# Local attention in a two-layer hybrid backbone: a score matmul of 64 partitions becomes one of 128

## The chip, the cores and the metric

The kernel runs on one core of one Trainium2 chip. The metric is the device time of one execution in microseconds (us). The kernel before took 3382.59 us (median of three runs, 3379.35 to 3383.43).

## What is computed

Two layers over 1152 tokens (1024 latent tokens on a grid and 128 context tokens, model width 1024). Each layer normalises and modulates its input, projects it once, runs three mixers side by side (a gated linear recurrence, a latent attention called MLA below, and a windowed attention called SWA or local attention), merges them through gates and adds the result to the residual. The change lies in the scores of the local attention of the latent tokens:

```python
def swa_latent(q, k, v, k_ctx, v_ctx, sink):
    ...
    def block(args):
        n, q_b = args
        start = n * BLOCK
        k_b = lax.dynamic_slice_in_dim(kp, start, 3 * BLOCK, axis=1)
        ...
        k_all = jnp.concatenate([k_b, k_ctx], axis=1)
        ...
        s = jnp.einsum("bqhgd,bkhd->bhgqk", q_b, k_all).astype(jnp.float32) * scale
        s = jnp.where(valid, s, NEG_INF)
        pr = sink_softmax(s, sink).astype(v.dtype)
        return jnp.einsum("bhgqk,bkhd->bqhgd", pr, v_all)
```

A query block of 128 tokens sees its own block of keys, the one before, the one after (masked to a band of 128) and the 128 context keys. There are 8 query heads of 64 channels, in two groups of four that share a key head. Context tokens attend to context tokens alone.

## The kernel before, in words

Every product is made in float32r from two parts: a value x is split into a high part xh (a cast to float32r) and a low part xl = x - xh. Most products are then three matmuls that add into one PSUM tile (`mm3`, line 239). The local attention does it with two, since its channel count, 64, is half of the 128 partitions. Keys are put side by side twice before they are transposed, so a transposed key tile `skt` holds the same 64 channels in partitions 0 to 63 and again in 64 to 127. `kprep_ops` (lines 1320 to 1343) writes the high parts of both halves to `KH[g]` on ScalarE (line 1337; the tile is `skh` in the profile) and the low parts of the lower half alone to `KL[g]` on VectorE (line 1341, `skl`). Its three steps are called `kp`, `ka`, `kb`. `qprep_ops` does it otherwise for the queries: the tile `qt` holds qh in partitions 0 to 63 and ql in 64 to 127 (lines 1351 to 1361).

`soft_ops(n, g)` makes the scores of query block n (0 to 8, of which 8 is the context block) and key head g. Its step `s0` to `s3` (function `mm`, lines 1379 to 1392) makes one head's scores in a PSUM tile `ss`. For each run of neighbouring key blocks it issues

- line 1388: `qt` (all 128 partitions) times `KH`, which is qh*kh + ql*kh;
- line 1389: `qt[0:64]` times `KL[0:64]`, which is qh*kl;
- line 1391: for each edge block a 128x128 matmul of the identity with the mask.

Blocks n = 1 to 5 have two runs, one of 384 columns with two masks and one of 128 columns (the context keys); block 0 has 256 with one mask and 128; block 6 has one run of 512 with two masks; block 7 one of 384 with one mask; block 8 one of 128. Over 8 heads and 2 layers these are 144 score steps with 240 matmuls of line 1388 and 240 of line 1389: 96 of 384 columns, 16 of 512, 16 of 256 and 112 of 128. In the profile the shape of a matmul is written rows*columns of the stationary operand and then rows x columns of the moving one, so line 1389 reads `64*128 64x384`.

After a score step VectorE takes the row maximum (`r`, line 1397) and bounds it by the sink (`b`, line 1401), ScalarE makes the exponentials (`x`, line 1406), VectorE and ScalarE make the inverse sums (`z1` to `z4`), and GpSimd scales the weights (`n`, line 1411). Then TensorE transposes them (`T`, line 1437), ScalarE and VectorE split them (`h`, line 1441, and `l`, line 1445), and TensorE multiplies them with the values (`V`, lines 1450 and 1451). Between these steps stand merge matmuls of the MLA branch (`m` and `e`, tile `mg`, line 239).

The order of all these steps on TensorE, ScalarE, VectorE and GpSimd is written out by hand, in the strings `MS_ORDER` (line 51, from the last MLA heads into the local attention) and `S_ORDER` (line 77, one turn per query block and key head), and the scheduler may not move them (line 1591). Three `ss` tiles are in turn.

Of the kernel before, what the change touches and what calls it, by code (L numbers as in the profile page):

```python
# [12 lines left out]
ALU = mybir.AluOpType  # L13
# [178 lines left out]
def _backbone(ctx, tc, nc, a, depth):  # L192
# [11 lines left out]
    def f(x):  # L204
        return x.bitcast(F32)
# [295 lines left out]
    for l in range(depth):  # L501
# [384 lines left out]
        with ExitStack() as ast:  # L886
# [197 lines left out]
            def w_ops(h):  # L1084
                r = []
                r.append(("uq", h, a["w_uq"][l, h], 3, P))
                if h and h % 2 == 0:
                    r.append(("uk", h // 2, a["w_uk"][l, h // 2], 2, P))
                if h in (0, 5):
                    r.append(("uv", h // 5, a["w_uv"][l, h // 5], 2, 256))  # L1090
                raws = []

                def load():
                    for nm, i, src, nk, n in r:
                        raws.append(wraw(src, nk, n, f"{nm}{l}_{i}"))

                def hi():
                    for (nm, i, src, nk, n), raw in zip(r, raws):
                        st[nm, i] = whl(nk, n, f"{nm}{l}_{i}")
                        nc.scalar.copy(out=st[nm, i][0], in_=raw)  # L1100

                def lo():
                    for (nm, i, src, nk, n), raw in zip(r, raws):
                        wh, wl = st[nm, i]
                        nc.gpsimd.tensor_tensor(out=wl, in0=raw, in1=f(wh), op=ALU.subtract)
                return {"w": hi, "wl": lo}, load
# [152 lines left out]
            for u in range(32):  # L1259
                h, pr = u // 4, u % 4  # L1260
                o = score_ops(h, pr)
# [13 lines left out]
            for h in (0, 1):  # L1275
                o, load = w_ops(h)
# [6 lines left out]
            KH, KL, VV = [None] * 2, [None] * 2, [None] * 2  # L1283
# [19 lines left out]
            def k_load(i):  # L1303
                if i > 7:
                    return
                kk = box["sqa"].tile([P, 512], F32, tag="kk", name=f"kk{l}_{i}", bufs=3)
                kraw_s[i] = kk
                if i > 4:
                    kk = kk.rearrange("p (t e) -> p t e", t=4)
                    if i < 7:  # L1310
                        nc.sync.dma_start(out=kk, in_=kv_d[4 * i - 20:4 * i - 16].rearrange("t p e -> p t e")[:, :, P:2 * P])
                    for t in (8, 9) if i == 7 else ():
                        nc.sync.dma_start(out=kk[:, t - 8], in_=kv_src(t)[1])
                    return
                kk = kk.rearrange("p (t g r e) -> p t g r e", t=2, g=2, r=2)
                for t in range(2):
                    for e in range(2):
                        nc.sync.dma_start(out=kk[:, t, :, e, :], in_=kv_src(K_OF[i] + t)[0].rearrange("p (g e) -> p g e", g=2))

            def kprep_ops(i):  # L1320
                r = {}
                cs = slice(K_OF[i] * P, (K_OF[i] + 2) * P)

                def mm():
                    r["ps"] = psd.tile([P, 512], F32, tag="d", name=f"skt{l}_{i}")
                    for g in range(2):
                        for e in range(2):
                            o = (2 * g + e) * P
                            nc.tensor.transpose(r["ps"][:, o:o + P], kraw_s[i][:, 256 * e + 128 * g:256 * e + 128 * g + 128], ident)
                    k_load(i + 3)  # L1330

                def hi():
                    for g in range(2):
                        if i == 0:
                            KH[g] = kkp.tile([P, 1280], F32R, tag=f"kh{g}", name=f"skh{l}_{g}")
                            KL[g] = kkp.tile([P, 1280], F32R, tag=f"kl{g}", name=f"skl{l}_{g}")
                        nc.scalar.copy(out=KH[g][:, cs], in_=r["ps"][:, 256 * g:256 * g + 256])

                def lo():
                    for g in range(2):  # L1340
                        nc.vector.tensor_tensor(out=KL[g][0:64, cs], in0=r["ps"][0:64, 256 * g:256 * g + 256],
                                                in1=f(KH[g][0:64, cs]), op=ALU.subtract)
                return {"kp": mm, "ka": hi, "kb": lo}

            def qprep_ops(t, g):
# [18 lines left out]
            def blocks_of(n):  # L1364
                return [b for b in (n - 1, n, n + 1) if 0 <= b < 8] + [8] if n < 8 else [9]

            def soft_ops(n, g):
                blocks = blocks_of(n)
                w = len(blocks) * P
                r, pts = {}, []  # L1370
                soft[n, g] = pts
                runs = []
                for i, b in enumerate(blocks):
                    if runs and runs[-1][1] + runs[-1][2] == b:
                        runs[-1][2] += 1
                    else:
                        runs.append([i, b, 1])

                def mm(j):
                    s = box["ps"].tile([P, 512], F32, tag="s", name=f"ss{l}_{n}_{4 * g + j}", bufs=3)  # L1380
                    r["s", j] = s
                    q = qt[n, g][:, j * P:(j + 1) * P]
                    for i, b, cnt in runs:
                        o = s[:, i * P:(i + cnt) * P]
                        ks = slice(b * P, (b + cnt) * P)
                        msk = [(ii, blocks[ii]) for ii in range(i, i + cnt)
                               if n < 8 and blocks[ii] < 8 and abs(blocks[ii] - n) == 1]
                        nc.tensor.matmul(o, q, KH[g][:, ks], start=True, stop=False)
                        nc.tensor.matmul(o, q[0:64], KL[g][0:64, ks], start=False, stop=not msk)
                        for z, (ii, bb) in enumerate(msk):  # L1390
                            nc.tensor.matmul(s[:, ii * P:(ii + 1) * P], ident_r, mask[:, 0 if bb == n - 1 else 1, :],
                                             start=False, stop=z == len(msk) - 1)

                def rmax(j):
                    if j == 0:
                        r["mx"] = box["sqa"].tile([P, 4, 4], F32, tag="mx", name=f"smx{l}_{n}_{g}", bufs=4)
                    nc.vector.tensor_reduce(out=r["mx"][:, 0, j:j + 1], in_=r["s", j][:, 0:w], axis=AX.X, op=ALU.max)

                def low(j):
                    h, mx = 4 * g + j, r["mx"]  # L1400
                    nc.vector.tensor_scalar(out=mx[:, 0, j:j + 1], in0=mx[:, 0, j:j + 1], scalar1=box["snk"][:, h:h + 1],
                                            scalar2=-1.0, op0=ALU.max, op1=ALU.mult)

                def exp(j):
                    pt = box["sqa"].tile([P, 512], F32, tag="pt", name=f"spt{l}_{n}_{4 * g + j}", bufs=12)
                    nc.scalar.activation(out=pt[:, 0:w], in_=r["s", j][:, 0:w], func=ACT.Exp, bias=r["mx"][:, 0, j:j + 1],
                                         accum_out=r["mx"][:, 1, j:j + 1])
                    pts.append(pt)

                def norm(j):  # L1410
                    nc.gpsimd.tensor_scalar(out=pts[j][:, 0:w], in0=pts[j][:, 0:w], scalar1=r["mx"][:, 3, j:j + 1],
                                            scalar2=1.0, op0=ALU.mult, op1=ALU.mult)

                o = {
                    "z1": lambda: nc.vector.tensor_tensor(out=r["mx"][:, 2], in0=box["snk"][:, 4 * g:4 * g + 4], in1=r["mx"][:, 0], op=ALU.add),
                    "z2": lambda: nc.scalar.activation(out=r["mx"][:, 2], in_=r["mx"][:, 2], func=ACT.Exp),
                    "z3": lambda: nc.vector.tensor_tensor(out=r["mx"][:, 1], in0=r["mx"][:, 1], in1=r["mx"][:, 2], op=ALU.add),
                    "z4": lambda: nc.vector.reciprocal(out=r["mx"][:, 3], in_=r["mx"][:, 1]),
                }
                for t, fn_ in (("s", mm), ("r", rmax), ("b", low), ("x", exp), ("n", norm)):  # L1420
                    o.update({f"{t}{j}": lambda fn_=fn_, j=j: fn_(j) for j in range(4)})
                return o
# [503 lines left out]
```

## Time and profile before

| | before |
|---|---|
| median of three runs | 3382.59 us (3379.35 to 3383.43) |
| profiled execution, first to last instruction | 3375.3 us |
| mean granted TensorE clock | 0.984 |
| TensorE matmuls busy | 3287.6 us (97%) |
| TensorE weight loads busy | 3095.7 us (92%) |
| VectorE busy | 1820.3 us (54%) |
| ScalarE busy | 1551.6 us (46%) |
| GpSimd busy | 1450.9 us (43%) |
| local attention of layer 0, first to last score matmul | from about 1335 to 1538 us |
| the same in layer 1 | from about 2979 to 3177 us |

The profiled execution's own device time is not listed apart from the three runs; they lie 4 to 8 us above its span, which is what lies around the first and the last instruction. A matmul's time in the profile runs until its results are written and overlaps with the next matmul's, so the pace of TensorE is read from the distance between two starts, not from the busy time. PE is TensorE's matmul row, PEld its row of weight loads.

### The profile page before, as it was taken

Reading aid. Unit: us, or ns where it says so; the run is one execution under the profiler, and the core shown is the slowest. Engines: PE = TensorE matmul, PEld = TensorE weight load, DVE = VectorE, ACT = ScalarE, POOL = GpSimd, SP = SyncE. Lnnn points to the kernel's source line nnn. Section 1 sums busy time; section 2 is a strip of 40 time slices with the busy share of each in tenths; the row PEclk is TensorE's granted clock in tenths of the full one; section 3 lists DMA queues with packets and bytes.
Section 4 is the critical chain, followed back from the end, with each engine's and each line's share of the span. In section 5 each row is a group of like instructions: output and inputs, shape, how many; then the busy total and the mean of one; then the engine's idle time right before and its main releaser. Section 6 shows DMA issues by size and latency. Waiting matters only on the chain. (4 is left out here: it accounts for less than half of the span.)

```text
span 3375.3 us, 52189 instructions
## 1 busy us (share of the span) xinstructions
PE 3287.6 (97%) x19572; PEld 3095.7 (92%) x19572; DVE 1820.3 (54%) x3254; ACT 1551.6 (46%) x3061; POOL 1450.9 (43%) x1174
## 2 busy tenths in 40 slices
PE   7999999999999999999999999999999999999998
PEld 4999999999998998778989999999999999977898
DVE  6345443332327888667563444423332588876766
ACT  4344444434226777554243433333341477765532
POOL 3655554433214444445374445333331244434543
PEclk9999999999999999899999999999999999989999
DMA  5333232232441002446432222222244200234563
GB/s 209 100 99 97 95 119 92 94 99 94 153 155 30 25 25 68 125 135 229 169 114 91 77 79 81 81 73 82 85 132 135 86 28 27 51 103 119 171 201 134
DMA packets 246652, 351.06 MB, mean 104 GB/s; under 512 B 73216, under 2 KB 200832, under 8 KB 246144
## 3 DMA queue, kind: packets, MB, share of 16 engines
q1 hardware_dynamic: 246400, 347.74, 32.5%
q8 instruction: 154, 2.52, 0.3%
q14 instruction: 98, 0.80, 0.1%
HBM read 248.88 MB, written 98.78 MB: 103 GB/s over the span
## 5 line engine op out<-in xcount | busy, mean ns | idle before, releaser
L239 PE MATMUL in<-hhi,wh_in 128*128 128x384 f32 x1536 | 524.0, 341 | 6.0 <-ACT osg L734 4.4
L239 PE MATMUL in<-hli,wh_in 128*128 128x384 f32 x1536 | 522.6, 340 | 1.6 <-DVE hli L427 1.6
L239 PE MATMUL in<-hhi,wl_in 128*128 128x384 f32 x1536 | 521.9, 340 | 0.0
L215 POOL TENSOR_TENSOR wl_in<-wr_in,wh_in 128x1024 fp32r<-128x1024 f32 x94 | 235.4, 2506 | 329.3 <-ACT wh_in L209 254.1
L239 PEld LDWEIGHTS in<-hhi,wh_in 128*128 128x128 f32 x1536 | 290.0, 189 | 6.8 <-ACT osg L734 5.0
L239 PEld LDWEIGHTS in<-hli,wh_in 128*128 128x128 f32 x1536 | 289.8, 189 | 3.9 <-DVE hli L427 3.9
L239 PEld LDWEIGHTS in<-hhi,wl_in 128*128 128x128 f32 x1536 | 289.9, 189 | 0.0
L239 PE MATMUL in<-hlh,wh_in 128*128 128x384 f32 x768 | 261.6, 341 | 2.8 <-DVE hlh L427 2.8
L239 PE MATMUL in<-hhh,wl_in 128*128 128x384 f32 x768 | 261.3, 340 | 2.0 <-POOL wl_in L215 2.0
L239 PE MATMUL in<-hhh,wh_in 128*128 128x384 f32 x768 | 261.5, 340 | 0.3 <-ACT osg L734 0.3
L1169 POOL TENSOR_SCALAR p<-p,mx 128x1152 f32<-128x1152 f32 x128 | 158.2, 1236 | 200.9 <-DVE mx L1166 126.4
L1220 DVE TENSOR_TENSOR pl<-pt,ph 128x512 fp32r<-128x512 f32 (+1 forms) x320 | 201.4, 636 | 29.8 <-ACT ph L1216 27.1
L1216 ACT CAST ph<-pt 128x512 fp32r<-128x512 f32 (+1 forms) x320 | 170.1, 552 | 92.4 <-PE pt L1209 87.9
L610 DVE SCALAR_TENSOR_TENSOR r<-r,txl 128x1156 f32<-128x1156 f32 x16 | 31.4, 1962 | 320.9 <-ACT r L609 320.9
L1209 PE MATMUL pt<-ident,p 128*128 128x128 f32 x1152 | 169.7, 274 | 9.5 <-DVE kl L1079 4.1
L734 ACT ACTIVATE osg<-in 128x384 f32<-128x384 f32 x144 | 69.0, 489 | 237.3 <-PE in L239 154.9
L1209 PEld LDWEIGHTS pt<-ident,p 128*128 128x128 f32 x1152 | 133.2, 141 | 32.6 <-DVE pl L1220 10.5
L209 ACT CAST wh_in<-wr_in 128x1024 fp32r<-128x1024 f32 x96 | 99.9, 1044 | 126.2 <-PE in L239 91.6
L1234 PE MATMUL o<-ph,v 128*128 128x256 f32 x576 | 153.2, 293 | 0.0
L239 PEld LDWEIGHTS in<-hlh,wh_in 128*128 128x128 f32 x768 | 145.0, 189 | 4.3 <-DVE hlh L427 4.3
L239 PEld LDWEIGHTS in<-hhh,wl_in 128*128 128x128 f32 x768 | 144.9, 189 | 2.3 <-POOL wl_in L215 2.3
L1234 PE MATMUL o<-pl,v 128*128 128x256 f32 x576 | 145.7, 280 | 0.0
(451 smaller groups left out, 9652.5 us busy)
## 6 DMA issues: line engine op xcount, KB each, us to landing
wr_in<-in_w_fm SPq DMA_DIRECT2D x96, 512.0 KB, 3.6
sg<-osg SPq DMA_DIRECT2D x144, 192.0 KB, 1.9
wr_wm<-in_w_mod SPq DMA_DIRECT2D x32, 512.0 KB, 4.0
wr_wo<-in_w_out SPq DMA_DIRECT2D x32, 512.0 KB, 3.7
yr<-gsil SPq DMA_DIRECT2D x16, 576.0 KB, 2.8
msgrnn<-sg SPq DMA_DIRECT2D x48, 192.0 KB, 2.4
u<-msgrnn SPq DMA_DIRECT2D x48, 192.0 KB, 2.5
qr<-qs SPq DMA_DIRECT2D x36, 256.0 KB, 3.9
```

Of the source, the lines that this page charges most:

```text
L209: nc.scalar.copy(out=hi, in_=src)
L215: eng.tensor_tensor(out=lo, in0=src, in1=f(hi), op=ALU.subtract)
L239: nc.tensor.matmul(ps, x, y, start=n == 0, stop=n == last)
L610: nc.vector.scalar_tensor_tensor(out=rr[d], in0=rr[d], scalar=1.0, in1=tt[d], op0=ALU.add, op1=ALU.mult)
L734: nc.scalar.activation(out=o, in_=ps, func=ACT.Sigmoid)
L1169: nc.gpsimd.tensor_scalar(out=pts[i], in0=pts[i], scalar1=mxs[i][:, 5:6], scalar2=1.0, op0=ALU.mult, op1=ALU.mult)
L1209: nc.tensor.transpose(ps[:, w:w + P], pts[q][:, k * P:(k + 1) * P], ident)
L1216: nc.scalar.copy(out=r["h", j][:, 0:width(j)], in_=r["t", j][:, 0:width(j)])
L1220: nc.vector.tensor_tensor(out=r["l", j][:, 0:width(j)], in0=r["t", j][:, 0:width(j)], in1=f(r["h", j][:, 0:width(j)]), op=ALU.subtract)
L1234: nc.tensor.matmul(O[:, 0:256], V[k][:, h % 4, :], x[:, 256 * i:256 * i + 256], start=k == 0 and e == 0, stop=k == 8 and e == 1)
```

## The change

The low parts of the keys are written to all 128 partitions of `KL`, and the second score matmul takes all 128 partitions of the queries and of `KL`. As both halves of the key tile are the same channels, the second matmul then gives qh*kl + ql*kl; the term ql*kl was left out before.

```diff
                 def lo():
                     for g in range(2):
-                        nc.vector.tensor_tensor(out=KL[g][0:64, cs], in0=r["ps"][0:64, 256 * g:256 * g + 256],
-                                                in1=f(KH[g][0:64, cs]), op=ALU.subtract)
+                        nc.vector.tensor_tensor(out=KL[g][:, cs], in0=r["ps"][:, 256 * g:256 * g + 256],
+                                                in1=f(KH[g][:, cs]), op=ALU.subtract)
...
                         nc.tensor.matmul(o, q, KH[g][:, ks], start=True, stop=False)
-                        nc.tensor.matmul(o, q[0:64], KL[g][0:64, ks], start=False, stop=not msk)
+                        nc.tensor.matmul(o, q, KL[g][:, ks], start=False, stop=not msk)
```

No instruction is added, removed or moved on any engine. What differs in the order of VectorE is the shape of the 20 subtractions of line 1341, here the first two of layer 0 in the last MLA heads (`skl` are the low parts, `qt` the queries, `mx` the row maxima of the MLA softmax):

```order
 L1361 TENSOR_TENSOR qt_0_0_12829<-sqt_0_0_12824,qt_0_0_12829 64x512
-L1341 TENSOR_TENSOR skl_0_12850<-skt_0_12839,skh_0_12849 64x256
-L1341 TENSOR_TENSOR skl_1_12853<-skt_0_12839,skh_1_12852 64x256
+L1341 TENSOR_TENSOR skl_0_12850<-skt_0_12839,skh_0_12849 128x256
+L1341 TENSOR_TENSOR skl_1_12853<-skt_0_12839,skh_1_12852 128x256
 L1146 TENSOR_REDUCE mx_7_1_0_12817<-sm_8907 128x1
```

They stand in the same place and now take 128 partitions of 256 elements instead of 64.

## Rows read from the trace of the kernel before

**Rows 1.** The page: the span, and the granted clock in 40 equal slices, in tenths.

```profile
span 3375.3 us, 52189 instructions
...
PEclk9999999999999999899999999999999999989999
```

**Rows 2.** Busy time by stretch, both local attentions: start:end, length, engines, granted clock, DMA.

```profile
1335.00:1538.00 203.00, 203.00 (x1046) 160.30 (x1045) 139.98 (x318) 114.28 (x275) 92.39 (x108) 0.94 0.42 126
2979.00:3177.00 198.00, 198.00 (x1021) 155.99 (x1019) 135.86 (x309) 111.57 (x269) 91.76 (x107) 0.94 0.43 127
```

**Rows 3.** Weight loads by line and shape: busy, mean ns, idle before them.

```profile
L1388 PEld LDWEIGHTS ss<-skh,qt 128*128 128x128 f32 x240 | 48.8, 203 | 3.1
L1389 PEld LDWEIGHTS ss<-skl,qt 64*128 64x128 f32 x240 | 46.4, 193 | 37.0 <-issue 26.7
...
L1391 PEld LDWEIGHTS ss<-mask,ident_r 128*128 128x128 f32 x224 | 37.0, 201 | 25.5 <-issue 23.4
```

**Rows 4.** Timeline of TensorE, a score step at full clock: start, length, instruction.

```profile
3014.35 0.42 PE L1388 MATMUL ss<-skh,qt 128*128 128x384 f32 x1
3014.70 0.43 PE L1389 MATMUL ss<-skl,qt 64*128 64x384 f32 x1
3015.06 0.44 PE L1391 MATMUL ss<-mask,ident_r 128*128 128x128 f32 x2
3015.34 0.28 PE L1388 MATMUL ss<-skh,qt 128*128 128x128 f32 x1
3015.55 0.32 PE L1389 MATMUL ss<-skl,qt 64*128 64x128 f32 x1
3015.80 0.44 PE L1388 MATMUL ss<-skh,qt 128*128 128x384 f32 x1
3016.17 0.44 PE L1389 MATMUL ss<-skl,qt 64*128 64x384 f32 x1
```

**Rows 5.** Timeline of TensorE, MLA scores of 128 partitions behind two transposes.

```profile
2930.28 0.42 PE L239 MATMUL sb<-kh,qh 128*128 128x384 f32 x1
2930.54 0.34 PE L239 MATMUL sb<-kl,qh 128*128 128x384 f32 x1
2930.72 0.34 PE L239 MATMUL sb<-kh,ql 128*128 128x384 f32 x1
2930.89 0.28 PE L1234 MATMUL o<-ph,v 128*128 128x256 f32 x1
2931.01 0.28 PE L1234 MATMUL o<-pl,v 128*128 128x256 f32 x1
```

**Rows 6.** Timeline of the weight loads, the load for the second of these.

```profile
2930.37 0.19 PEld L239 LDWEIGHTS sb<-kl,qh 128*128 128x128 f32 x1
```

**Rows 7.** Timeline of TensorE, first matmuls of two score steps at half clock.

```profile
3005.13 0.67 PE L1388 MATMUL ss<-skh,qt 128*128 128x384 f32 x1
...
3007.58 0.69 PE L1388 MATMUL ss<-skh,qt 128*128 128x384 f32 x1
```

**Rows 8.** Busy time by stretch: late MLA (two), then early local attention; columns as before.

```profile
1260.00:1300.00 40.00, 40.00 (x290) 37.91 (x289) 35.97 (x82) 30.22 (x76) 19.80 (x20) 1.00 0.24 57
1300.00:1320.00 20.00, 18.96 (x140) 16.96 (x139) 19.08 (x43) 15.33 (x37) 6.57 (x6) 1.00 0.45 100
1340.00:1400.00 60.00, 60.00 (x270) 45.67 (x269) 40.39 (x92) 34.22 (x82) 19.61 (x21) 0.80 0.40 122
2980.00:3050.00 70.00, 70.00 (x319) 53.26 (x319) 47.48 (x107) 39.41 (x95) 27.66 (x32) 0.83 0.36 108
```

**Rows 9.** Line 1389 alone in two stretches: TensorE, its weight loads, clock.

```profile
1340.00:1400.00 60.00, 18.39 (x43) 9.00 (x42) 0.80 0.40 122
...
2980.00:3050.00 70.00, 21.11 (x50) 10.37 (x50) 0.83 0.36 108
```

**Rows 10.** VectorE by line and shape: 64 and 128 partitions of 256 elements.

```profile
L1220 DVE TENSOR_TENSOR pl<-pt,ph 128x256 fp32r<-128x256 f32 x48 | 19.8, 413 | 1.0 <-ACT ph L1216 0.7
...
L1341 DVE TENSOR_TENSOR skl<-skt,skh 64x256 fp32r<-64x256 f32 x20 | 7.4, 409 | 0.1
```

## The prediction

> **What bounds the kernel now.** The page comes first: of the 3375.3 us the two local attentions fill the 16th to the 19th and the 36th to the 38th of its 40 slices, and in each of them one slice (the 17th and the 36th) has a lower granted clock than all others [rows 1]. The busy time by stretch is next: between the first and the last score matmul TensorE is busy in 203.00 of 203.00 us in layer 0 and 198.00 of 198.00 in layer 1, VectorE, the next, in 139.98 and 135.86 [rows 2]. So TensorE sets the pace of this stage, and a microsecond taken from its queue is gained as long as VectorE can follow.
>
> But busy is not full pace. The weight loads tell: the loader stood idle for 37.0 us ahead of the 240 loads of line 1389, the only ones of 64 rows in this stage, and 25.5 us ahead of the 224 of the masks behind them, mostly put down to "issue" (no other engine to wait for); ahead of the 240 loads of line 1388 it was 3.1 us [rows 3]. A load that comes late makes its matmul late. The timeline of one step shows how much.
>
> **What a 64-row matmul costs now.** Line 1388's 384 columns start at 3014.35, line 1389's at 3014.70, the masks at 3015.06, the pair of 128 columns at 3015.34 and 3015.55, the next step at 3015.80 [rows 4]: 0.35, 0.36, 0.28, 0.21 and 0.25, in all 1.45 us. The MLA scores are the nearest picture of what the change makes of it: two matmuls of 384 columns that load the same 128-row queries twice. Behind transposes the first takes 0.26 us until the next start, the second 0.18, a third 0.17, and one of 256 columns 0.12 [rows 5]; the load for the second began at 2930.37, while the first ran until 2930.70 [rows 5, 6]. There the loads hide.
>
> A step of 128 rows is priced from these: the first 384 columns 0.26 (this step too stands behind transposes), the second 0.18, two masks and the two matmuls of 128 columns at most 0.12 each, as a matmul of 256 columns takes that. That is 0.26 + 0.18 + 4 x 0.12 = 0.92 us, 0.53 less. The matmul behind a step pays as well: the next step's first 384 columns take 0.37 (3015.80 to 3016.17) instead of the 0.26 or 0.18 of rows 5, at least 0.10 more. So a step with two 64-row matmuls loses 0.63 us, 0.315 for each, and both its parts have the same pattern in it (a late start in, a late start out), so I take 0.315 for all 240: **76 us**. Ends: 62.5 us, the idle time of the loader alone (37.0 + 25.5) [rows 3], and 80, with 0.11 for a matmul of 128 columns.
>
> **The clock.** The granted clock is 0.80 in 1340 to 1400 and 0.83 in 2980 to 3050 [rows 8]. Half clock (1.2 GHz) gives 0.5, so 0.40 x 60 = 24 and 0.34 x 70 = 23.8 us were at half, 47.8 together, and in both layers this begins in the first, densest run of score steps. A step there takes 2.45 us (3005.13 to 3007.58) [rows 7] against 1.45. If the clock stays full, 47.8 x 1.00 / 2.45 = **20 us** come on top. Bounds: 0, if it falls just as long, and 24, half of 47.8.
>
> **What is given back.** By the sum the first stretch gets short for VectorE. In 1340 to 1400 lie 43 of the 64-row matmuls [rows 9]: 13.5 us less, and 10 for the clock, leave TensorE 60 - 23.5 = 36.5 us, while VectorE has 40.39 us to do; in 2980 to 3050 they are 50, which leaves 44 us against 47.48 [rows 8]. So 4 + 3.5 us cannot be had, and TensorE will wait for maxima and for the low parts of the weights. How tight the two can be packed is seen in the MLA: with VectorE busy 35.97 of 40 us (90%) TensorE never stopped, with 19.08 of 20 (95%) it was idle for 1.04 us, 5% [rows 8]. The later part has slack: 1400 to 1538 keeps at most 139.98 - 40.39 = 99.6 us of VectorE, and TensorE needs 138 - 77 x 0.315 = 114 (the rest of layer 0's 120 matmuls). But the order is fixed by hand, and waits of single steps will show. I put 5% on the early parts, 4 us, and half of 5% on the later ones, 6 us: **18 us** in all. Ends: 7.5 and 35.
>
> The subtractions of line 1341 cost nothing: VectorE takes 413 ns for 128 partitions of 256 elements and 409 for 64 [rows 10]; 20 x 4 ns. Nothing is moved past any queue.
>
> **A rule that speaks against it.** In rows 6 a load of 128 rows runs beside a matmul of 128 rows. The Trainium skill, "TensorE: Matmul & The Clock Gate", Part 3 ("What overlaps and what doesn't"), says that a weight load overlaps with a running matmul only when the two use different row groups. By that rule loads of 128 rows would always wait, and the change would give about nothing (3382 us); the trace disagrees, with 0.18 us from start to start where the load alone is 0.19.
>
> **Sum.** 76 + 20 - 18 = 78 us. The span of the profiled execution lies 7.3 us under the median of the runs, and nothing around the span changes, so the median goes from 3382.6 to about **3305 us**.
>
> **Rivals.**
> - *The clock does not come back.* TensorE's new waits for VectorE in the first steps keep it at half for as long. For it: VectorE is short there by the sum. Against it: in 1300 to 1320, where TensorE has such waits too, the clock stayed at 1.00 [rows 8]. Then 76 - 18 = 58 us: 3325 us. If the waits reach their far end as well, 76 - 35 = 41: 3342 us.
> - *Nothing waits.* The order has enough lead everywhere, and a matmul of 128 columns takes 0.11: 80 + 24 less 4 = 100 us, 3283 us. For it: ahead of scores and transposes VectorE is the one that waits now.
> - *The pause is not the row count.* It could come from two matmuls on the same queries or the same PSUM tile, and would stay. Against it: the MLA pair does both without a pause [rows 5]. Then the time is 3382 us, or 2 us more if the weight load goes from 193 to 203 ns [rows 3]. That the low parts don't reach the upper half, and the change does nothing, is excluded by the shape in the order.
> - *Slower.* TensorE, quicker than its suppliers, stops so often that the granted clock is at half in most of the stage. Half clock costs a step 1.00 us of 2.45, so each us at half costs 0.41. It would decide from 58 / 0.41 = 141 us at half beyond today's 47.8, about half of the 401 us; with 200 more, 3382.6 + 82 - 58 = 3407 us. Against it: the late MLA has VectorE as busy, and full clock.
>
> **Chances.** The forecast 58%, the clock at half 25% and with far waits 6%, nothing waits 7%, no effect 2%, slower 2%. The range reaches from 3284, just above "nothing waits", to 3334, above the clock rival and short of its far end. A measurement of this kernel tells 0.2% (7 us) from no change: faster 0.96, same 0.02, slower 0.02.
>
> **What would show it.** Line 1389 should read 128*128, the idle time ahead of its loads and of the masks' should fall from 37.0 and 25.5 to a few us, a full-clock step from 1.45 to about 0.92. Both stages should get some 38 us shorter, VectorE in them near 90% busy, and TensorE should show waits for VectorE or ScalarE, first around 1340 to 1380; the clock in the first 60 us should be above 0.80. I am wrong on the cause if the idle time ahead of line 1389 stays, on the clock if it stays near 0.80, and on the give-back if the stage loses over 30 us to waits.

## The result, and the profile after

The changed kernel takes 3290.71 us (median of four runs, 3289.32 to 3291.54) against 3381.73 us for the kernel before in the same comparison (3379.35 to 3383.43): a ratio of 0.9733, 95% interval 0.9719 to 0.9747, 91 us less. The forecast was 3305 us, with a range of 3284 to 3334.

The page of the changed kernel: the span, TensorE and its weight loads, and the granted clock in 40 slices.

```profile
span 3287.5 us, 52185 instructions
...
PE 3194.6 (97%) x19572; PEld 3065.0 (93%) x19572; DVE 1812.6 (55%) x3254; ACT 1549.2 (47%) x3061; POOL 1451.2 (44%) x1174
...
PEclk9999999999999999999999999999999999999999
```

The span is 87.8 us shorter, and the two slices with a lower clock [rows 1] are gone. The medians differ by 3 us more, since the profiled execution of the kernel before was a quick one: wherever a run lists both, its device time is 1.8 us above its span (3289.32 and 3287.5 for the changed kernel), so that execution took about 3377 us, and the 4 to 8 us given above are for the most part the spread of its runs. Where the time went is read from the first and the last score matmul of each layer. The view of line 1388 by itself gives the starts of its weight loads; first the kernel before, layer 0 and layer 1 (duration min/median/max in ns, then first and last start in us).

```profile
L1388 PEld LDWEIGHTS ss<-skh,qt x120: 186/190/337, 1335.2 to 1535.7; 128*128 128x128 f32 x120
...
L1388 PEld LDWEIGHTS ss<-skh,qt x120: 186/190/337, 2976.1 to 3176.6; 128*128 128x128 f32 x120
```

The same two views of the changed kernel.

```profile
L1388 PEld LDWEIGHTS ss<-skh,qt x120: 186/190/192, 1337.0 to 1493.8; 128*128 128x128 f32 x120
...
L1388 PEld LDWEIGHTS ss<-skh,qt x120: 186/190/192, 2933.8 to 3090.6; 128*128 128x128 f32 x120
```

The stage fell from 200.5 to 156.8 us in both layers, 43.7 each (in layer 1 the stage begins at 2976.1, 3 us before the stretch of [rows 2]). Twice that is 87.4 of the 87.8 us: all but 0.4 us was won there, and ahead of the first and behind the second stage the times moved by 1.8 us, in opposite directions.

The weight loads by line and shape, to be held against [rows 3]:

```profile
L1389 PEld LDWEIGHTS ss<-skl,qt 128*128 128x128 f32 x240 | 45.9, 191 | 1.0
L1388 PEld LDWEIGHTS ss<-skh,qt 128*128 128x128 f32 x240 | 45.6, 190 | 7.4 <-ACT spt L1406 6.2
L1391 PEld LDWEIGHTS ss<-mask,ident_r 128*128 128x128 f32 x224 | 41.2, 188 | 1.5
```

The idle time ahead of line 1389 went from 37.0 to 1.0 us, ahead of the masks from 25.5 to 1.5. What grew is ahead of line 1388: 7.4 us instead of 3.1, of which 6.2 are a new wait, for ScalarE's exponentials. A step with two runs behind transposes, which took 1.45 us [rows 4], in the timeline of TensorE:

```profile
2988.78 0.42 PE L1388 MATMUL ss<-skh,qt 128*128 128x384 f32 x1
2989.04 0.34 PE L1389 MATMUL ss<-skl,qt 128*128 128x384 f32 x1
2989.22 0.33 PE L1391 MATMUL ss<-mask,ident_r 128*128 128x128 f32 x2
2989.39 0.27 PE L1388 MATMUL ss<-skh,qt 128*128 128x128 f32 x1
2989.50 0.27 PE L1389 MATMUL ss<-skl,qt 128*128 128x128 f32 x1
2989.61 0.45 PE L1450 MATMUL so<-sph,svv 128*128 128x512 f32 x1
```

Starts lie 0.26, 0.18, 0.17 (two masks), 0.11 and 0.11 us apart: 0.83 us in all. In the weight loads the one for line 1389 begins while the matmul of line 1388 (2988.78 to 2989.20) runs:

```profile
2988.87 0.19 PEld L1389 LDWEIGHTS ss<-skl,qt 128*128 128x128 f32 x1
```

The other engines and the clock by stretch: the stage of layer 0 and that of layer 1, then the first part of layer 0's and its rest (start:end, length, PE, PEld, DVE, ACT, POOL busy, granted clock, DMA share, GB/s).

```profile
1337.00:1494.00 157.00, 153.45 (x1034) 142.57 (x1032) 133.25 (x311) 111.51 (x271) 92.15 (x107) 1.00 0.52 157
2934.00:3091.00 157.00, 153.44 (x1033) 142.55 (x1032) 133.40 (x312) 111.50 (x272) 92.17 (x107) 1.00 0.53 156
1340.00:1400.00 60.00, 56.49 (x394) 52.38 (x393) 55.06 (x125) 46.19 (x112) 34.28 (x37) 1.00 0.48 144
1400.00:1494.00 94.00, 94.00 (x618) 87.43 (x616) 75.70 (x183) 62.66 (x155) 57.73 (x70) 1.00 0.57 170
```

The clock is full throughout; in the first 60 us it was 0.80 [rows 8]. TensorE is now idle for 3.55 us of layer 0's stage (3.56 in layer 1), and 3.51 of these lie in the first 60 us, where VectorE is busy in 55.06 us (92%). In the other 94 us VectorE is busy for 81% and TensorE never stops. The three largest waits of TensorE in layer 0's stage (who waited for whom, us in total, times, longest):

```profile
PE ss L1388 <- ACT spt L1406: 2.2, 5, 0.8
PE spt L1437 <- DVE spl L1445: 0.6, 1, 0.6
PE spt L1437 <- DVE smx L1417: 0.3, 1, 0.3
```

The longest total is the scores' wait for a free `ss` tile: three are in turn, and a tile is free when ScalarE has made its exponentials. ScalarE in turn waited there for VectorE's bounded maxima (line 1401), from 1337 to 1400:

```profile
ACT spt L1406 <- DVE smx L1401: 3.0, 6, 0.9
```

### The profile page after: what moved, and what is told of

Same layout as the page of the kernel before. It is cut to its first block, busy times and chain, and to the rows that moved or that the text cites. A ratio compares the mean times of both kernels' runs of the same rounds, so it can differ in the third digit from the quotient of the medians.

```text
span 3287.5 us, 52185 instructions
## 1 busy us (share of the span) xinstructions
PE 3194.6 (97%) x19572; PEld 3065.0 (93%) x19572; DVE 1812.6 (55%) x3254; ACT 1549.2 (47%) x3061; POOL 1451.2 (44%) x1174
```

## The experiments

Each ran beside the kernel before on the same chip; the ratio is to that kernel's runs there. The diffs are against the changed kernel.

**The VectorE half alone** (`e1_low_only`).

```diff
-                        nc.tensor.matmul(o, q, KL[g][:, ks], start=False, stop=not msk)
+                        nc.tensor.matmul(o, q[0:64], KL[g][0:64, ks], start=False, stop=not msk)
```

> The low parts of the keys are written to all 128 partitions, but the second score matmul stays at 64. Theory (the gain comes from the matmul's row count alone): no change, 3382 us within 7; the 20 subtractions take about 413 ns each instead of 409; 37 us of idle time ahead of the loads of line 1389 as before. Rival (something of the gain or a cost lies in the VectorE part): 3374 us or less, or 3390 or more.

Measured: 3378.49 us against 3380.15, a ratio of 1.0 (0.9987 to 1.0014). The subtractions and the loads of line 1389:

```profile
L1341 DVE TENSOR_TENSOR skl<-skt,skh 128x256 fp32r<-128x256 f32 x20 | 7.5, 416 | 0.1
...
L1389 PEld LDWEIGHTS ss<-skl,qt 64*128 64x128 f32 x240 | 46.5, 194 | 37.0 <-issue 26.6
```

With twice the partitions a subtraction takes 416 ns instead of 409, and the idle time of the loader stays. The gain lies in the matmul: the VectorE part alone changes the time by less than the noise.

**96 rows instead of 128** (`e4_rows96`).

```diff
-                        nc.tensor.matmul(o, q, KL[g][:, ks], start=False, stop=not msk)
+                        nc.tensor.matmul(o, q[0:96], KL[g][0:96, ks], start=False, stop=not msk)
```

> The second score matmul takes 96 rows; of the term ql*kl only 32 of the 64 channels are then added. Theory (TensorE stops when it changes between a 64-row setting and the full array, and 96 rows need the full array): as with 128 rows, 3291 us, no idle time ahead of the loads of line 1389, a full-clock step of 384 + 128 columns in about 0.8 us. Rival (the cost is in every row that is missing of 128): halfway, about 3336 us. Second rival (any number but 128 pays in full): 3382 us.

Measured: 3293.45 us, ratio 0.9737 (0.9718 to 0.9755), the same as the change. The loads:

```profile
L1389 PEld LDWEIGHTS ss<-skl,qt 96*128 96x128 f32 x240 | 47.2, 197 | 1.0
```

Layer 0's stage, at full clock, takes 157.1 us, against 156.8 with 128 rows. The full 128 rows are not needed, and the cost does not grow with the rows that are missing: 96 rows show no pause, 64 pay all. This also rules out that two matmuls on the same queries or on the same PSUM tile cause the pause, since both are still there.

This run shows one thing more. Its layer 1 took 161.3 us, 4.2 more than layer 0, and there the clock fell, though no matmul of the stage has 64 rows:

```profile
2943.00:2948.00 5.00, 4.19 (x35) 3.92 (x35) 4.42 (x14) 4.16 (x13) 2.67 (x4) 1.00 0.37 84
2948.00:2953.00 5.00, 4.83 (x23) 4.49 (x22) 4.77 (x13) 2.82 (x9) 2.78 (x4) 0.58 1.01 332
2953.00:2958.00 5.00, 5.00 (x24) 5.00 (x24) 2.79 (x9) 4.04 (x9) 1.84 (x4) 0.50 0.95 332
```

Ahead of it TensorE was busy in 4.19 of 5 us, with a wait of 0.8 us for an `ss` tile. The changed kernel has like waits (2.2 us for `ss` tiles in each stage) and kept the full clock in both. So the waits that the change brings may cost the clock in one execution and not in another; why it fell in this one is open.

**64 rows, but side by side** (`e6_grouped64`). In a step with two runs the two 64-row matmuls stand next to each other; the sums are those of the kernel before.

```diff
-                    for i, b, cnt in runs:
+                    for z, (i, b, cnt) in enumerate(runs):
...
+                        if z == 0:
                             nc.tensor.matmul(o, q, KH[g][:, ks], start=True, stop=False)
+                            for ii, bb in msk:
+                                nc.tensor.matmul(s[:, ii * P:(ii + 1) * P], ident_r, mask[:, 0 if bb == n - 1 else 1, :],
+                                                 start=False, stop=False)
+                            nc.tensor.matmul(o, q[0:64], KL[g][0:64, ks], start=False, stop=True)
+                        else:
+                            nc.tensor.matmul(o, q[0:64], KL[g][0:64, ks], start=True, stop=False)
+                            nc.tensor.matmul(o, q, KH[g][:, ks], start=False, stop=True)
```

> Still 64 rows, but in steps with two runs the two 64-row matmuls stand side by side: 384 of KH, masks, 384 of KL, 128 of KL, 128 of KH. The changes between 64 and 128 rows fall from 480 to 288. Theory (the cost is paid per change of the setting, about 0.33 us for an entry and an exit): 96 x 0.33 = 32 us less, and 0 to 20 from the clock: 3330 to 3350 us; the second of the two 64-row loads has no idle time ahead of it. Rival (each matmul of 64 rows pays for itself): 3382 us within 7.

Measured: 3337.0 us, ratio 0.9866 (0.985 to 0.9882), 43 us less than before. A step behind transposes, with lines 1393 and 1395 the 64-row matmuls, 1389, 1391 and 1396 the 128-row ones:

```profile
1445.02 0.42 PE L1389 MATMUL ss<-skh,qt 128*128 128x384 f32 x1
1445.28 0.33 PE L1391 MATMUL ss<-mask,ident_r 128*128 128x128 f32 x2
1445.54 0.44 PE L1393 MATMUL ss<-skl,qt 64*128 64x384 f32 x1
1445.83 0.22 PE L1395 MATMUL ss<-skl,qt 64*128 64x128 f32 x1
1445.97 0.33 PE L1396 MATMUL ss<-skh,qt 128*128 128x128 f32 x1
```

The next matmul starts at 1446.13, so the step takes 1.11 us, between the 1.45 of the kernel before and the 0.83 of the changed one. The weight loads of the four lines:

```profile
L1389 PEld LDWEIGHTS ss<-skh,qt 128*128 128x128 f32 x144 | 28.7, 199 | 2.9 <-ACT spt L1410 1.6
L1393 PEld LDWEIGHTS ss<-skl,qt 64*128 64x128 f32 x144 | 27.4, 190 | 12.3 <-issue 0.8
L1395 PEld LDWEIGHTS ss<-skl,qt 64*128 64x128 f32 x96 | 19.5, 203 | 0.0
L1396 PEld LDWEIGHTS ss<-skh,qt 128*128 128x128 f32 x96 | 19.0, 198 | 13.0 <-issue 2.5
```

The loader waits when rows change, into 64 (12.3 us) and out again (13.0), and not at all (0.0) between two loads of 64 rows. So the price is for the change into 64 rows and out again, and not for each 64-row matmul; a change between 128 and 96 rows has none, by the 96-row run. The Trainium skill, "TensorEngine Tiling (Array Packing)", Key Properties, says that TensorE drains when its tiling mode changes. The waits of the loader at these changes agree with it. With 96 changes in and 96 out removed, 32 us were forecast and 0 to 20 from the clock; the gain was 43 us, and the clock in 1340 to 1400 is 0.89 here, between 0.80 and 1.00.

**The early and the late query blocks apart** (`e2_early`, `e3_late`).

```diff
-                        nc.tensor.matmul(o, q, KL[g][:, ks], start=False, stop=not msk)
+                        h_ = P if n < 3 else 64
+                        nc.tensor.matmul(o, q[0:h_], KL[g][0:h_, ks], start=False, stop=not msk)
```

The late run has `n >= 3` in its place.

> 128 rows in the second score matmul of query blocks 0 to 2 alone (96 of the 240), 64 rows in the others. Theory (0.33 us for each 64-row matmul, and 20 us from the clock that fell in the first dense run of them, less some 8 us of waits): 32 + 20 - 8 = 44 us, 3338 us; granted clock 1.0 in 1340 to 1400. Rival (the clock is no part of the gain, or falls all the same): 3350 us or more, clock near 0.80 in the early part or in a later one.

> The other half: 128 rows in query blocks 3 to 8 (144 of the 240), 64 rows in blocks 0 to 2. Theory: 144 x 0.33 = 48 us, no gain from the clock, which stays near 0.80 in 1340 to 1400: 3334 us, and the gains of this run and of the early one add up to the whole, 91 us. Rival (the clock looks at the whole of the stage, so that it rises here too): 3320 us or less, clock above 0.9 in the early part.

Measured: early 3342.68 us, ratio 0.9881 (0.986 to 0.9902), 39.5 us less than before; late 3330.59 us, ratio 0.9849 (0.9828 to 0.987), 51.6 us less. Together that is 91.1, the whole, though each of the two is only known to some 7 us. The first 60 us of layer 0's stage in the early run:

```profile
1340.00:1400.00 60.00, 56.50 (x353) 49.11 (x353) 51.60 (x116) 42.25 (x103) 30.32 (x33) 0.97 0.45 135
```

and in the late run:

```profile
1340.00:1400.00 60.00, 60.00 (x266) 45.10 (x266) 40.24 (x90) 34.34 (x83) 19.76 (x21) 0.80 0.41 122
```

The clock goes with the early blocks: 0.97 where these take 128 rows, 0.80 where they don't, whatever the late ones do. A full clock was expected for the early run; the missing 0.03 is one stretch at half, from 1386.6 to 1390.0, right behind its first three steps with 64-row matmuls (1381.74 to 1386.15). The changes of rows are not the only thing that decides, though: in the 96-row run the clock fell without them. In the late run layer 0 is a clean measure of the price, since its early part is as before and TensorE never waits there:

```profile
L1388 PEld LDWEIGHTS ss<-skh,qt x120: 186/190/337, 1336.2 to 1512.8; 128*128 128x128 f32 x120
```

The stage takes 176.6 us instead of 200.5: 23.9 us for 72 matmuls, **0.33 us each**. (Layer 1 gained 22.3 us; there the clock was at half for 3.4 us more than in the kernel before.)

**The grouped order with 128 rows** (`e7_grouped128`): the diff of the grouped run, with `q` and `KL[g][:, ks]` in place of the halves.

> The same order as in the grouped run, with 128 rows: a step is KH wide, masks, KL wide, KL narrow, KH narrow. Theory (in the changed kernel a narrow matmul takes 0.11 us because its weight load takes that long, and one that follows a wide matmul can take 0.06, since its load had time): 0.05 us in each of the 96 steps with two runs, so 3286 us, 5 less than the change alone. Rival (the stage is held by VectorE and ScalarE by now): no difference to the change, 3291 us within 4.

Measured: 3294.95 us, ratio 0.9745 (0.9727 to 0.9762): no gain over the change. Its stages take 156.7 us, against 156.8. A step behind transposes:

```profile
2991.33 0.42 PE L1389 MATMUL ss<-skh,qt 128*128 128x384 f32 x1
2991.59 0.33 PE L1391 MATMUL ss<-mask,ident_r 128*128 128x128 f32 x2
2991.76 0.39 PE L1393 MATMUL ss<-skl,qt 128*128 128x384 f32 x1
2991.99 0.22 PE L1395 MATMUL ss<-skl,qt 128*128 128x128 f32 x1
2992.05 0.27 PE L1396 MATMUL ss<-skh,qt 128*128 128x128 f32 x1
2992.16 0.45 PE L1454 MATMUL so<-sph,svv 128*128 128x512 f32 x1
```

The narrow matmul behind the wide one did take 0.06 us, as expected, but the wide one behind the masks takes 0.23 instead of 0.18, and the step is 0.83 us as in the changed kernel. Both orders have the same six loads. The expectation failed, and the rival beside it is not shown either: the step itself did not get shorter, so nothing had to be held by VectorE.

## Why the prediction was right, point by point

- *TensorE sets the pace, and the time is won in its queue.* Right: 87.4 of 87.8 us of the span are won between the first and the last score matmul, and none is lost behind them.
- *A 64-row matmul costs 0.315 us, 76 us in all.* Right and a little low: 0.33 measured in the late run, 240 x 0.33 = 80 us, the upper bound of the forecast. Two masks take 0.17 instead of the 0.24 that a matmul of 256 columns suggested, and a narrow matmul 0.11 instead of 0.12. The cause, which the prediction left as "a late start in, a late start out", is now shown to be the change into 64 rows and out again.
- *The clock, 20 us.* Right, in this kernel's runs. The size can be had from the trace of the kernel before alone. Each distance between two starts in its half-clock stretches is held against the median distance of the same matmul, between the same neighbours, at full clock. The 47.6 us at half would have taken 27.6 at full clock: 20 us, 10 in each layer. By the same medians the whole stage of layer 0 would take 190.2 us instead of 200.5, so they rebuild what lies outside these stretches to 0.2 us. That the clock came back hangs for the most part on the early blocks (early and late run), but it was not certain, as layer 1 of the 96-row run shows.
- *Given back, 18 us.* This is the term that was mis-sized, and with the first one it makes most of the difference between the 78 us of the sum and the 87.4 us of the two stages (the rest of the 14 us between the forecast and the median is the spread noted above). A layer won 43.7 us; 39.8 (120 x 0.33) and 10 less 43.7 leaves 6.1 us given back. TensorE's idle time, 3.55 us a layer, shows only part of it; the rest are matmuls that start late while the one before still counts as busy. The medians of the changed kernel say where: its first 48 matmuls of line 1388 (blocks 0 to 2) take 44.8 us instead of 38.9, 5.8 more, and the other 72 take 112.0 instead of 111.6. Early that is 11.7 us for both layers, against 11.5 forecast (the shortage of 7.5 and 4 more), by the chain that was expected, from VectorE's maxima by way of ScalarE's exponentials, with VectorE busy for 92% of the first 60 us. Later it is under 1 us, against 6 forecast: with VectorE at 81% TensorE never stopped. The order by hand had enough lead.
- *The signs.* VectorE was expected near 90% busy in both stages. It is 85% (133.25 of 157.00 us), and over 90% only in the first 60 us.
- *A rule against it.* The weight load runs beside the matmul of the same 128 rows (2988.87 inside 2988.78 to 2989.20), as [rows 6] had shown, and starts lie 0.18 us apart with loads of 0.19. The sentence of the Trainium skill, "TensorE: Matmul & The Clock Gate", Part 3, that a load overlaps with a running matmul only when their row groups differ, does not agree with these rows.
- *The rivals.* That the pause is not the row count fell with the 96-row and the grouped run. The clock at half fell with the profile after, though the 96-row run shows some of it in one layer. "Nothing waits" came nearest (3283 us): the later part went its way, the early part did not.

The sum with measured terms: 80 from the late run, 20 from the kernel before at half clock, and 12 to 13 given back, from the changed kernel: 80 + 20 - 12.5 = 87.5 us, against 87.4 in the two stages. The 80 is worked out from 72 of the 240 matmuls, and the other two are estimates from median distances.

## What to carry to other kernels

Here a weight load of 64 rows next to 128-row matmuls, with "issue" as the end of its idle time, was the mark of a cost that no busy time shows. To see such a cost, compare the distances of starts with those of a stretch where all matmuls have 128 rows. Where a matmul with half the partitions stands between full ones, and the other half can be filled with something useful or harmless, fill it: here the added rows cost TensorE nothing that shows, and each subtraction on VectorE 7 ns. If that can't be, set the 64-row matmuls side by side; it brought nearly half of the gain here, 43 of 91 us. Then look at the engines behind TensorE: where VectorE had no slack, 12 of 100 us were given back.

## What was not expected of the hardware

A matmul of 96 rows costs what one of 128 costs, with no pause that shows, so the price has a step between 64 and 96 rows, and no slope between 96 and 128. And the second of two masks, on the same identity, starts 0.06 us behind the first (0.17 less 0.11 for the pair), half of what narrow matmuls take whose loads follow each other closely: in these steps a narrow matmul took less behind a wide one than behind another narrow one, and the grouped order moved that cost within a step without removing it.
